# Column mean of an 8192 x 8192 matrix: an eight-row ring with two-row adds in place of five two-row slabs, and a head that comes uncast by the hardware queue

## The chip, the cores and the metric

The kernel runs on one core of one Trainium2 chip. The metric is the device time of one execution in microseconds, as the median of repeated executions.

## The reference

```python
def reference(x: np.ndarray) -> np.ndarray:
    return np.mean(x, axis=0)
```

`x` is an 8192 x 8192 fp32 matrix (268 MB) of normal random numbers. The result is one row of 8192 fp32 means. Each element of x is read once and added once, so the work is a stream from HBM with one addition for each element.

## The kernel before, in words

The 8192 rows of x are taken as 64 blocks of 128 rows ("rows" of the schedule, below). A block of 128 rows lies across the 128 partitions, with all 8192 columns along each partition. The sum over the rows is made in two steps: first the blocks are added elementwise, which leaves 128 partial sums per column, then TensorE multiplies with a vector of ones, which adds up the 128 partitions.

**Loads.** `load` (L87) fetches two blocks at a time with a DMA issued by GpSimd, which casts fp32 to bf16 on the way into a slab of 128 x 16384 bf16. Each partition takes two neighbouring rows of x, one contiguous run of 64 KB. There are five slabs (`bufs=5`), so a load waits until the slab of five loads earlier has been consumed.

**Adds.** `total` is a 128 x 8192 fp32 tile. It is cleared once (L56). VectorE adds every block to it with one `tensor_add` of 8192 elements per partition (L96), 61 times, two for each slab. The loop runs over 31 two-block loads; of the last of these VectorE takes only the first block.

**TensorE.** `add_chunks` (L76) adds a stretch of columns of a source into PSUM with a matmul whose weights are ones: `ones_b` for bf16 sources, `ones` for the fp32 `total`. `BLOCKS` divides the 8192 columns into seven blocks, each with one PSUM bank `acc`. A block (c0, w, g) has g chunks of w columns; chunk j goes to partitions 32 j to 32 j + 31 of the bank, that is, to its own group of 32 columns of the TensorE array. TensorE takes, in this order: the second block of the last two-block load; `total`; the last but one row block, loaded alone; and the last row block, loaded in six pieces of falling width (L136), 4096 columns to 128. The instructions stand in TensorE's queue in that order, and no later one passes an earlier one.

**Drains and stores.** When a piece of the last row block has been added, `drain` scales a bank by 1/8192 into `res`, on ScalarE for blocks 1, 3 and 5 (L113) and on VectorE for the others (L115). `store` writes it to HBM, on ScalarE's queue or on SyncE's (L125, and L123 for the last block).

Nothing here is planned by hand beyond the order of the program: each engine executes its own instructions in that order, and waits on semaphores for the tiles that it reads or overwrites.

Of the kernel before, what the change touches and what calls it, by code (L numbers as in the profile page):

```python
# [1 line left out]

# [4 lines left out]


@with_exitstack
def kernel(  # L10
    ctx: ExitStack,
    tc: tile.TileContext,
    x: bass.AP,
    out: bass.AP,
):

    nc = tc.nc
    P = nc.NUM_PARTITIONS
    R, C = x.shape
    F32, BF16 = mybir.dt.float32, mybir.dt.bfloat16
    assert (R, C) == (8192, 8192)
    inv_r = 1.0 / float(R)
    G = 4
    M = P // G
    K = 2  # L30
    N_GROUPS = R // (K * P)

    BLOCKS = [
        (0, 512, 4), (2048, 512, 4), (4096, 512, 4), (6144, 256, 4), (7168, 128, 4),
        (7680, 128, 3), (8064, 128, 1),
    ]

    const_pool = ctx.enter_context(tc.tile_pool(name="const", bufs=1))  # L40
    slab_pool = ctx.enter_context(tc.tile_pool(name="slab", bufs=5))
    sum_pool = ctx.enter_context(tc.tile_pool(name="sum", bufs=1))
    psum_pool = ctx.enter_context(
        tc.tile_pool(name="acc", bufs=1, space=bass.MemoryType.PSUM)
    )
    res_pool = ctx.enter_context(tc.tile_pool(name="res", bufs=1))

    ones = const_pool.tile([P, M], F32, tag="ones")
    nc.vector.memset(ones, 1.0)  # L49
    ones_b = const_pool.tile([P, M], BF16, tag="ones_b")  # L50
    nc.vector.memset(ones_b, 1.0)  # L51
    warm = const_pool.tile([P, M], F32, tag="warm")
    nc.scalar.mul(out=warm, in_=ones, mul=inv_r)  # L53

    total = sum_pool.tile([P, C], F32, tag="total")
    nc.vector.memset(total, 0.0)  # L56

    acc = [
        psum_pool.tile([P, 512], F32, name=f"acc{b}", tag=f"acc{b}")
        for b in range(len(BLOCKS))  # L60
    ]
    res = [
        res_pool.tile([P, w], F32, name=f"res{b}", tag=f"res{b}")
        for b, (_, w, _) in enumerate(BLOCKS)
    ]
    started = [[False] * g for _, _, g in BLOCKS]

    def add_chunks(src, lo, hi, b, cast=True, stop=False):

        c0, w, g = BLOCKS[b]  # L70
        for j in range(g):
            c = c0 + j * w
            if not lo <= c < hi:
                continue
            assert c + w <= hi
            nc.tensor.matmul(  # L76
                out=acc[b][j * M : (j + 1) * M, 0:w],
                lhsT=ones_b if cast else ones,
                rhs=src[:, c : c + w],
                start=not started[b][j],  # L80
                stop=stop,
            )
            started[b][j] = True

    def load(r0, k):
        t = slab_pool.tile([P, K * C], BF16, name="slab", tag="slab")
        nc.gpsimd.dma_start(  # L87
            out=t[:, 0 : k * C],
            in_=x[r0 : r0 + k * P, :].rearrange("(p k) c -> p (k c)", k=k),
        )  # L90
        return t

    for g in range(N_GROUPS - 1):
        t = load(g * K * P, K)
        for k in range(K if g < N_GROUPS - 2 else 1):
            nc.vector.tensor_add(out=total, in0=total, in1=t[:, k * C : (k + 1) * C])  # L96
    for b in range(len(BLOCKS)):
        add_chunks(t[:, C : 2 * C], 0, C, b)
    for b in range(len(BLOCKS)):
        add_chunks(total, 0, C, b, cast=False)  # L100
    t = load(R - K * P, 1)
    for b in range(len(BLOCKS)):
        add_chunks(t, 0, C, b)


    last = x[R - P : R, :]
    tb = slab_pool.tile([P, K * C], BF16, name="slab", tag="slab")

    def drain(b, eng):
        w = BLOCKS[b][1]  # L110
        rows = BLOCKS[b][2] * M
        if eng == "act":
            nc.scalar.mul(out=res[b][0:rows], in_=acc[b][0:rows, 0:w], mul=inv_r)  # L113
        else:
            nc.vector.tensor_scalar(  # L115
                out=res[b][0:rows], in0=acc[b][0:rows, 0:w], scalar1=inv_r, scalar2=None,
                op0=mybir.AluOpType.mult,
            )

    def store(b, q):  # L120
        lo, w, g = BLOCKS[b]
        if g == 1:
            q.dma_start(out=out[lo : lo + w], in_=res[b][0:1, :])  # L123
        else:
            q.dma_start(  # L125
                out=out[lo : lo + g * w].rearrange("(j w) -> j w", j=g),
                in_=res[b].rearrange("(j m) w -> j m w", m=M)[0:g, 0, :],
            )

    PIECES = ((0, 2), (2, 3), (3, 4), (4, 5), (5, 6), (6, 7))  # L130
    spans = []
    for b0, b1 in PIECES:
        lo = BLOCKS[b0][0]
        hi = BLOCKS[b1 - 1][0] + BLOCKS[b1 - 1][1] * BLOCKS[b1 - 1][2]
        spans.append((lo, hi))
        nc.gpsimd.dma_start(out=tb[:, lo:hi], in_=last[:, lo:hi])  # L136
    for (b0, b1), (lo, hi) in zip(PIECES, spans):
        for b in range(b0, b1):
            add_chunks(tb, lo, hi, b, stop=True)
            drain(b, "act" if b in (1, 3, 5) else "dve")  # L140
            store(b, nc.scalar if b in (1, 3, 5) else nc.sync)


# [1 line left out]
_INS = ['x']  # L145
_OUTS = [((8192,), 'float32')]


# [23 lines left out]
```

## Time and profile before

| | |
|---|---|
| median of 12 runs | 629.59 us (628.79 to 630.51) |
| the profiled execution's own time | 629.14 us |
| its span, first to last instruction | 627.3 us |
| VectorE busy | 539.2 us (86%), of it 61 adds of 8.69 us |
| TensorE busy | 11.0 us (2%) |
| GpSimd | 38 loads; HBM read 268.44 MB |
| granted TensorE clock | 0.998 |

The span is what the profile shows; the execution's own time also has 1.9 us around it. The page divides the span into 40 slices and gives for each engine its busy share in tenths, and for the DMA engines their mean busy share; it then follows the chain of work that ended last back to the start. In the timeline each line has a start, a duration, the engine, the line of the code and the operation, and in brackets how long the engine was idle before and what ended that.

### The profile page before, as it was taken

Reading aid. Unit: us, or ns where it says so; the run is one execution under the profiler, and the core shown is the slowest. Engines: PE = TensorE matmul, PEld = TensorE weight load, DVE = VectorE, ACT = ScalarE, POOL = GpSimd, SP = SyncE. Lnnn points to the kernel's source line nnn. Section 1 sums busy time; section 2 is a strip of 40 time slices with the busy share of each in tenths; the row PEclk is TensorE's granted clock in tenths of the full one; section 3 lists DMA queues with packets and bytes.
Section 4 is the critical chain, followed back from the end, with each engine's and each line's share of the span. In section 5 each row is a group of like instructions: output and inputs, shape, how many; then the busy total and the mean of one; then the engine's idle time right before and its main releaser. Section 6 shows DMA issues by size and latency. Waiting matters only on the chain.

```text
span 627.3 us, 466 instructions
## 1 busy us (share of the span) xinstructions
PE 11.0 (2%) x120; PEld 4.6 (1%) x120; DVE 539.2 (86%) x68; ACT 2.8 (0%) x5; POOL 20.4 (3%) x42
## 2 busy tenths in 40 slices
PE   0000000000000000000000000000000000000015
PEld 0000000000000000000000000000000000000002
DVE  4488988889888899888898888988889988899881
ACT  0000000000000000000000000000000000000000
POOL 1000000000000000000000000000000000000000
PEclk9999999999999999999999999999999999999999
DMA  9999999999999999999999999999999999999997
GB/s 190 211 219 215 217 217 211 224 211 224 209 226 207 228 205 230 201 234 201 234 201 234 201 234 201 235 201 234 201 234 201 234 201 234 201 235 201 234 200 138
DMA packets 5523, 134.29 MB, mean 214 GB/s; under 512 B 760, under 2 KB 1028, under 8 KB 1296
## 3 DMA queue, kind: packets, MB, share of 16 engines
q0 software_dynamic: 5472, 134.22, 99.7%
q1 hardware_dynamic: 26, 0.02, 0.0%
q8 instruction: 1, 0.02, 0.0%
q10 hardware_dynamic: 22, 0.01, 0.0%
q14 instruction: 2, 0.02, 0.0%
HBM read 268.44 MB, written 0.03 MB: 428 GB/s over the span
## 4 chain that ended last, share of the span: by engine, by line
DVE 82%; another core or an unknown queue 9%; DMA 7%; PE 1%; issue 1%; POOL 0%; DVEq 0%; POOLq 0%
DVE total L96 82%; DMA slab<-in_x_dram 7%; PE acc L76 1%; POOL slab L87 0%; DVEq L96 0%; DVE res L115 0%; POOLq L156 0%
## 5 line engine op out<-in xcount | busy, mean ns | idle before, releaser
L96 DVE TENSOR_TENSOR total<-total,slab 128x8192 f32<-128x8192 f32 x61 | 530.2, 8692 | 72.5 <-DMA slab<-in_x_dram 71.5
L87 POOL DMA_DIRECT2D slab<-in_x_dram x32 | 17.0, 535 | 527.0 <-DVE total L96 526.2
L76 PE MATMUL acc<-slab,ones_b 128*32 128x512 bf16 (+2 forms) x72 | 5.1, 369 | 606.4 <-DMA slab<-in_x_dram 606.4
L115 DVE TENSOR_SCALAR res<-acc 128x512 f32<-128x512 f32 (+2 forms) x4 | 2.0, 488 | 10.4 <-PE acc L76 10.3
L56 DVE MEMSET total<- 128x8192 f32 x1 | 6.9, 6885 | 1.7 <-issue 1.7
L76 PEld LDWEIGHTS <-ones_b 128*32 128x32 bf16 x72 | 2.8, 108 | 608.2 <-issue 606.8
L76 PE MATMUL acc<-total,ones 128*32 128x512 f32 (+2 forms) x48 | 6.4, 681 | 6.8 <-DVE total L96 6.8
L136 POOL DMA_DIRECT2D slab<-in_x_dram x6 | 3.2, 544 | 37.3 <-DVE total L96 18.8
L113 ACT ACTIVATE res<-acc 128x512 f32<-128x512 f32 (+2 forms) x3 | 1.3, 418 | 620.9 <-PE acc L76 620.9
L76 PEld LDWEIGHTS acc<-total,ones 128*32 128x32 f32 x48 | 2.0, 143 | 11.2 <-DVE total L96 7.1
L53 ACT ACT_TABLE_LOAD x1 | 1.3, 1283 | 0.7 <-PEq L156 0.7
L49 DVE MEMSET ones<- 128x32 f32 x1 | 0.1, 85 | 0.8 <-PEq L156 0.8
L53 ACT ACTIVATE warm<-ones 128x32 f32<-128x32 f32 x1 | 0.2, 229 | 0.0
L156 POOL MEMSET const-float32-0.0<- 128x1 f32 x1 | 0.1, 98 | 0.2 <-issue 0.2
L156 POOL MEMSET const-bfloat16-1.0<- 128x1 bf16 x1 | 0.1, 101 | 0.0
L156 POOL MEMSET const-float32-1.0<- 128x1 f32 x1 | 0.1, 98 | 0.0
L156 POOL MEMSET const-uint8-127<- 128x1 uint8 x1 | 0.1, 98 | 0.0
L51 DVE MEMSET ones_b<- 128x32 bf16 x1 | 0.1, 85 | 0.0
## 6 DMA issues: line engine op xcount, KB each, us to landing
slab<-in_x_dram POOLq DMA_DIRECT2D x31, 4096.0 KB, 78.8
slab<-in_x_dram POOLq DMA_DIRECT2D x1, 2048.0 KB, 69.2
slab<-in_x_dram POOLq DMA_DIRECT2D x1, 1024.0 KB, 54.7
slab<-in_x_dram POOLq DMA_DIRECT2D x1, 512.0 KB, 56.6
slab<-in_x_dram POOLq DMA_DIRECT2D x1, 256.0 KB, 57.4
slab<-in_x_dram POOLq DMA_DIRECT2D x1, 128.0 KB, 58.7
slab<-in_x_dram POOLq DMA_DIRECT2D x1, 96.0 KB, 58.4
slab<-in_x_dram POOLq DMA_DIRECT2D x1, 32.0 KB, 39.6
```

Source lines behind the costliest of these rows:

```text
L49: nc.vector.memset(ones, 1.0)
L51: nc.vector.memset(ones_b, 1.0)
L53: nc.scalar.mul(out=warm, in_=ones, mul=inv_r)
L56: nc.vector.memset(total, 0.0)
L76: nc.tensor.matmul(out=acc[b][j * M : (j + 1) * M, 0:w], lhsT=ones_b if cast else ones, rhs=src[:, c : c + w], start=not started[b][j], st ...
L87: nc.gpsimd.dma_start(out=t[:, 0 : k * C], in_=x[r0 : r0 + k * P, :].rearrange("(p k) c -> p (k c)", k=k),)
L96: nc.vector.tensor_add(out=total, in0=total, in1=t[:, k * C : (k + 1) * C])
L113: nc.scalar.mul(out=res[b][0:rows], in_=acc[b][0:rows, 0:w], mul=inv_r)
L115: nc.vector.tensor_scalar(out=res[b][0:rows], in0=acc[b][0:rows, 0:w], scalar1=inv_r, scalar2=None, op0=mybir.AluOpType.mult,)
L136: nc.gpsimd.dma_start(out=tb[:, lo:hi], in_=last[:, lo:hi])
L156: nc = _bacc.Bacc("TRN2", target_bir_lowering=False, num_devices=1)
```

## The change

- **Ring.** The slab pool is replaced by one tile `ring` of eight row blocks in bf16. Loads take consecutive places in it: eight loads of four blocks, fourteen of two, two of one (`LOADS`), then the last block in five pieces. A load waits until the places that it overwrites have been consumed.
- **Head.** The first row block comes first and alone. Its first 1024 columns are loaded as fp32 straight into `total` by two DMAs, one issued by SyncE and one by ScalarE, 64 partitions each. The other 7168 columns come by GpSimd as bf16 into place 7 of the ring, and ScalarE copies them into `total` (L98). The clearing of `total` and a warm-up activation on ScalarE are gone.
- **Two-row sum.** `total` is twice as wide, 128 x 16384 fp32. VectorE adds two row blocks with one `tensor_add` of 16384 elements per partition (L118), 27 times. The first four-block load makes the second half out of two blocks (L113) and adds the other two to the first half (L114, L115). Before the last two-block load that VectorE takes, the second half is added to the first (L122), and then the two blocks of that load one by one (L124).
- **TensorE's rows.** TensorE takes the two single-row loads and the last block: the first single row as it comes, then the first half of `total`, then the second single row (`late`), then the pieces of the last block.
- **Blocks.** `BLOCKS` has six entries in place of seven: three of 4 x 512 as before, then 2 x 512, 2 x 384 and 2 x 128. There are 18 chunks for each source instead of 24. TensorE's list of instructions has 116 rows where it had 153.
- **Stores.** Blocks 0 and 1 share a tile `res01` and one store on SyncE's queue (L169). Block 4 is stored from ScalarE's queue, the others from SyncE's (L148). Drains are at L139 (ScalarE: blocks 1, 3 and 4) and L141 (VectorE: blocks 0, 2 and 5); matmuls are at L86, loads at L97, L105 and L159.

```diff
-    K = 2
-    N_GROUPS = R // (K * P)
+    RING = 8
+    LOADS = [4] * 8 + [2] * 14 + [1] * 2
+    PE_ROWS = 2
+    HEADW = 1024
     BLOCKS = [
-        (0, 512, 4), (2048, 512, 4), (4096, 512, 4), (6144, 256, 4), (7168, 128, 4),
-        (7680, 128, 3), (8064, 128, 1),
+        (0, 512, 4), (2048, 512, 4), (4096, 512, 4), (6144, 512, 2), (7168, 384, 2),
+        (7936, 128, 2),
     ]
...
+    total = sum_pool.tile([P, 2 * C], F32, tag="total")
+    ring = ring_pool.tile([P, RING * C], BF16, tag="ring")
+    half = P // 2
+    nc.sync.dma_start(out=total[0:half, 0:HEADW], in_=x[0:half, 0:HEADW])
+    nc.scalar.dma_start(out=total[half:P, 0:HEADW], in_=x[half:P, 0:HEADW])
...
-    warm = const_pool.tile([P, M], F32, tag="warm")
-    nc.scalar.mul(out=warm, in_=ones, mul=inv_r)
-    total = sum_pool.tile([P, C], F32, tag="total")
-    nc.vector.memset(total, 0.0)
...
-    for g in range(N_GROUPS - 1):
-        t = load(g * K * P, K)
-        for k in range(K if g < N_GROUPS - 2 else 1):
-            nc.vector.tensor_add(out=total, in0=total, in1=t[:, k * C : (k + 1) * C])
-    for b in range(len(BLOCKS)):
-        add_chunks(t[:, C : 2 * C], 0, C, b)
-    for b in range(len(BLOCKS)):
-        add_chunks(total, 0, C, b, cast=False)
-    t = load(R - K * P, 1)
-    for b in range(len(BLOCKS)):
-        add_chunks(t, 0, C, b)
+    at = RING - 1
+    head = ring[:, at * C : (at + 1) * C]
+    nc.gpsimd.dma_start(out=head[:, HEADW:C], in_=x[0:P, HEADW:C])
+    nc.scalar.copy(out=total[:, HEADW:C], in_=head[:, HEADW:C])
+    lo_, hi_ = total[:, 0:C], total[:, C : 2 * C]
+    r0, at = P, 0
+    n_dve = len(LOADS) - PE_ROWS
+    for g, k in enumerate(LOADS):
+        t = ring[:, at * C : (at + k) * C]
+        nc.gpsimd.dma_start(
+            out=t,
+            in_=x[r0 : r0 + k * P, :].rearrange("(p k) c -> p (k c)", k=k),
+        )
+        r0 += k * P
+        at = (at + k) % RING
+        row = [t[:, i * C : (i + 1) * C] for i in range(k)]
+        if g == 0:
+            nc.vector.tensor_add(out=hi_, in0=row[1], in1=row[3])
+            nc.vector.tensor_add(out=lo_, in0=lo_, in1=row[0])
+            nc.vector.tensor_add(out=lo_, in0=lo_, in1=row[2])
+        elif g < n_dve - 1:
+            for i in range(0, k, 2):
+                nc.vector.tensor_add(
+                    out=total, in0=total, in1=t[:, i * C : (i + 2) * C]
+                )
+        elif g == n_dve - 1:
+            nc.vector.tensor_add(out=lo_, in0=lo_, in1=hi_)
+            for i in range(k):
+                nc.vector.tensor_add(out=lo_, in0=lo_, in1=row[i])
+        elif g == n_dve:
+            for b in range(len(BLOCKS)):
+                add_chunks(t, 0, C, b)
+        else:
+            late = t
...
-    PIECES = ((0, 2), (2, 3), (3, 4), (4, 5), (5, 6), (6, 7))
+    PIECES = ((0, 2), (2, 3), (3, 4), (4, 5), (5, 6))
...
+    for b in range(len(BLOCKS)):
+        add_chunks(lo_, 0, C, b, cast=False)
+    for b in range(len(BLOCKS)):
+        add_chunks(late, 0, C, b)
     for (b0, b1), (lo, hi) in zip(PIECES, spans):
         for b in range(b0, b1):
             add_chunks(tb, lo, hi, b, stop=True)
-            drain(b, "act" if b in (1, 3, 5) else "dve")
-            store(b, nc.scalar if b in (1, 3, 5) else nc.sync)
+            drain(b, "act" if b in (1, 3, 4) else "dve")
+            if b == 1:
+                nc.sync.dma_start(
+                    out=out[0 : 8 * 512].rearrange("(b j w) -> j b w", b=2, j=G),
+                    in_=res01.rearrange("(j m) b w -> j m b w", m=M)[:, 0, :, :],
+                )
+            elif b > 1:
+                store(b, nc.scalar if b == 4 else nc.sync)
```

## The prediction

> **What bounds the kernel now.** I read the page first, its slices and its chain of waits.
>
> ```profile
> DMA  9999999999999999999999999999999999999997
> PE 11.0 (2%) x120; PEld 4.6 (1%) x120; DVE 539.2 (86%) x68; ACT 2.8 (0%) x5; POOL 20.4 (3%) x42
> DVE 82%; another core or an unknown queue 9%; DMA 7%; PE 1%; issue 1%; POOL 0%; DVEq 0%; POOLq 0%
> L96 DVE TENSOR_TENSOR total<-total,slab 128x8192 f32<-128x8192 f32 x61 | 530.2, 8692 | 72.5 <-DMA slab<-in_x_dram 71.5
> ```
>
> The chain gives VectorE 82%, but that is only who stood in it: VectorE waits 71.5 us for slabs, and the DMA row is full to the last slice. The timeline of VectorE shows who sets the pace.
>
> ```profile
> 23.62 17.42 DVE L96 TENSOR_TENSOR total<-total,slab 128x8192 f32<-128x8192 f32 x2 [14.15 <-DMA slab<-in_x_dram]
> 42.90 17.42 DVE L96 TENSOR_TENSOR total<-total,slab 128x8192 f32<-128x8192 f32 x2 [1.86 <-DMA slab<-in_x_dram]
> ...
> 584.22 17.42 DVE L96 TENSOR_TENSOR total<-total,slab 128x8192 f32<-128x8192 f32 x2 [1.90 <-DMA slab<-in_x_dram]
> 603.53 8.69 DVE L96 TENSOR_TENSOR total<-total,slab 128x8192 f32<-128x8192 f32 x1 [1.89 <-DMA slab<-in_x_dram]
> ```
>
> From 42.90 to 603.53 lie 29 loads: 19.33 us for two row blocks ("rows" below: 128 rows of x, 4.19 MB), 9.66 us a row, 434 GB/s. VectorE needs 17.42 of each 19.33 us and idles 1.9. So **the loads bound the body**. The end is read from the timeline of TensorE, its weight loads and the stores.
>
> ```profile
> 612.27 0.20 PEld L76 LDWEIGHTS acc<-total,ones 128*32 128x32 f32 x8 [7.09 <-DVE total L96]
> 613.13 0.20 PEld L76 LDWEIGHTS acc<-total,ones 128*32 128x32 f32 x4 [0.66 <-issue]
> ...
> 617.40 0.88 PEld L76 LDWEIGHTS acc<-total,ones 128*32 128x32 f32 x19 [0.66 <-issue]
> 618.17 0.10 PEld L76 LDWEIGHTS <-ones_b 128*32 128x32 bf16 x3
> 619.86 0.69 DVE L115 TENSOR_SCALAR res<-acc 128x512 f32<-128x512 f32 x1 [7.63 <-PE acc L76]
> 620.07 0.60 ACT L113 ACTIVATE res<-acc 128x512 f32<-128x512 f32 x1 [617.81 <-PE acc L76]
> 623.64 0.60 PE L76 MATMUL acc<-slab,ones_b 128*32 128x128 bf16 x8 [1.61 <-DMA slab<-in_x_dram]
> 624.79 0.41 SPq L123 DMA_DIRECT2D out_dram<-res  x1
> ```
>
> VectorE's last add ends at 612.23, TensorE reduces `total` and the late row until about 619.3, and then still waits for the last pieces: the last lands at 623.6 and the span ends 3.7 us later (2.47 after the last store's issue at 624.79). VectorE was done 11.4 us before the last byte. **That slack hides its tail today**, and the change spends it.
>
> **What the Trainium skill says.** "VectorE: DVE Perf Modes", section on the TRN2 errata, prices an fp32 tensor_tensor at (N+151)/0.96 ns: 8.69 us for 8192, as the trace has it (8692 ns), so an estimated 17.22 us for 16384; its tier table keeps fp32 tensor_tensor at one element per cycle. "TensorE: Matmul & The Clock Gate", Part 1, has the array at half clock after idling and at full clock after some 3.4 us of work, with a free-running window. The trace agrees in kind: groups of four 512-wide fp32 passes start 0.855 us apart from 612.27 to 617.40; the eight 256-wide and sixteen 128-wide ones left, 1.71 us at that rate, start within 0.88. Here the switch came after 5.1 us. "DMA: Bandwidth & Descriptors", "Where 436 GB/s comes from", gives a ceiling of 435 GB/s; the trace has 434, so no load shape can gain much. Its "Specifications" gives a first byte after 1 us from GpSimd and 0.6 us from SP or ACT. The trace: GpSimd issues at 1.23 and the DMA share rises in the 2.5 to 2.6 window, 1.3 us; the last SP issue at 624.79 moves bytes in 625.8 to 625.9, 1.1 us.
>
> **The change, part by part.**
>
> *Start.* SP and ACT issue the first 1024 columns, 0.52 MB, 1.2 us of stream, by the hardware queue. They are free when the other engines start (ACT's table load at 0.73, VectorE at 0.81), so by 1.1 to 1.4 us later, bytes move at about 1.9 to 2.1 instead of 2.5. GpSimd's own first issue stays at 1.23. I take 0.6 us gained; the bounds are 0 (it starts no earlier) and 1.2 (the whole piece is hidden). The memset of `total` (6.9 us), the warm-up activation and its table load go: nothing, all lay under the first load's wait until 23.62. The new ScalarE copy of 7168 columns, at the 0.60 us per 512 of its evictions 8.4 us, starts when the head lands near 13 and ends near 21. GpSimd's third load waits for it, with every later load queued behind; but the first four-row load keeps the DMA engines busy until about 51, and the second add, which reads the copy, comes later still. Cost zero under that cover; with it gone, 8.4 us once.
>
> *Loads.* Same bytes, 30 GpSimd loads for 38. The 434 GB/s stands 0.3% under the ceiling, so fewer loads give between 0 and 0.4 us; I take 0. A four-row load (16.8 MB, two 64 KB runs per partition) shows nowhere in the trace; rate unchanged taken, 1% worse over 32 rows would be 3 us.
>
> *The ring in the four-row stage.* Before, five slabs; now two four-row halves. A half is freed 2 x 17.25 = 34.5 us after its load lands; the load in flight ends at 38.66. Cycle of a half: 34.5, 0.29 to GpSimd (VectorE ends 41.04, issue 41.34), 3.06 for a fresh start (1.23 to 23.62 less 19.33) and 38.66: 76.5 us against 77.3 for two loads of stream. **Slack 0.8 us**, cost zero. A doubled issue (0.53 more for twice the descriptors) still fits. The two-row loads have three loads of slack. VectorE, late when they begin, gains 2.1 us per load and has caught up by the ninth of 14.
>
> *The wide adds.* 61 x 8.69 = 530 us becomes 27 x 17.22 + 6 x 8.69 = 517 us. Covered by the loads: no gain.
>
> *The end of VectorE.* This is the term that counts. Now `total` is two rows wide and must be folded (L122), and three rows, not two, follow the last VectorE load. The second last two-row load completes row 59 of 64. Before, row 60 starts its add at 584.22; so row 59 at 584.22 - 9.66 - 0.6 = 573.96. Then one wide add 17.22, the fold 8.69, two adds of the last load 17.38 (it lands at 593.3, while the fold runs), gaps 0.14: 43.43 us, ending at **617.39, against 612.23**. TensorE's fp32 pass and, queued in order behind it, the late row and all the last pieces wait for that.
>
> *TensorE.* The fp32 pass shrinks from 24 to 18 matmuls of the same 8192 columns, but the last three blocks use two column groups, not four. Three blocks of 4x512 at half clock: 6 x 0.855 = 5.13 us, as before; then at full clock 2 x 0.427 for 512, 2 x 0.32 for 384, 2 x 0.11 for 128: 1.71. Sum 6.84, before 5.9. By when the clock rises (after 3.4 to 6.8 us), 6.0 to 7.7. From 617.43: ends 624.27. The late row takes 1.2 (618.17 to 619.3 before): the last pieces start at 625.5, all landed by about 623. They are not waited for any more.
>
> *Drains and stores.* Before, six pieces spread them; now they come together. After the start of the last pieces the first drain came 0.6 us later and ScalarE's 0.8: VectorE 626.1 (0.69), 626.8 (0.69), 627.5 (0.3); ScalarE 626.3 (0.6), 626.9 (0.6), 627.5 (0.5) and its store, issued at 628.1. SP issues four stores 0.54 us apart, the joint one from 626.95: the last at about 628.6. The end lies 2.47 later: **631.05, against 627.26: +3.8 us**. Fewer blocks and stores save nothing I can place, since the queue of drains sets the end.
>
> *Sum.* Start -0.6; VectorE's tail 43.43 less the 9.66 of one row and the 28.01 from row 60's start to 612.23, +5.8; TensorE's fp32 pass +0.9; from the late row's end to the span's end 5.55 us (625.5 to 631.05) for 8.0 (619.3 to 627.3), since no piece is waited for, -2.4: +3.7, 3.8 unrounded. The profiled execution took 629.14 (span 627.3 and 1.9 around it), 0.45 under the median 629.59. So 632.9 there, 633.4 at the median; I say 633.3.
>
> **The rivals.**
>
> *The ring starves (slower still).* If the first bytes of a four-row load come d us later than a two-row one's, each half's cycle overruns by d - 0.8, half of that per load, over six loads: d = 2 gives 3.6 us, 637. Or the longer runs stream 1% slower: 636. For it: 0.8 us is thin. Against: the issue takes only 0.53 us, the descriptors are of the size used now, and the queue is never empty at the hand-over. Chance 0.12.
>
> *The fold is cheap (not slower).* The fold's operands are all fp32, a form absent from the trace. If it ran at two elements per cycle, 4.35 us instead of 8.69, VectorE would end at 613.0 and the time fall to 633.3 - 4.35 = 629.0, 0.1% under before. It decides from 3.8 us off VectorE's 43.4. For it: nothing measured; against: the skill's tier table and the fp32 operand and result of today's adds at 8692 ns. Together with a full 1.2 us at the start it would be 628.4. Chance 0.08.
>
> *The hardware loads do not start earlier.* Then the head is plain: 633.9. It lies inside the forecast's range.
>
> **How the numbers follow.** Forecast 0.80, its own range 631.8 to 635.0 (start 0.6 either way, clock 0.85, stores 0.5). Starving 0.12, cheap fold 0.08. About 0.2% (1.26 us) is what a measurement of this kernel can tell from no change; the cheap fold splits into 0.04 faster and 0.04 the same, and the rest of the cases are slower; I move 0.02 more to no change for a lucky sum of bounds: faster 0.04, same 0.06, slower 0.90. The range 631.2 to 636.8 holds the forecast and most of the starving case.
>
> **What would show it.** Right: the fold at 8.7 us and wide adds at 17.2; the last add ending near 617.4; TensorE's fp32 pass beginning then and its last pieces waiting for no DMA; the last store's issue near 628.6; in the four-row stage a DMA share near 1 and landings 38.7 us apart; first bytes near 2.0. Wrong: gaps in the DMA share when two halves change over, a fold near 4.4 us, or a last VectorE add before 613, with TensorE again waiting for the last pieces.

## Result and the profile after

The changed kernel takes **636.53 us** (median, 635.48 to 636.82) against 629.55: 1.0107 of the time before, 95% interval 1.0098 to 1.0117. That is slower by 7.0 us, where 3.7 were forecast; the direction holds, and so does the wide range (631.2 to 636.8), but only because most of the starving case was taken into it: the forecast's own range, 631.8 to 635.0, does not hold 636.53. The profiled execution took 637.36 us, 0.8 above the median, with a span of 635.2.

The page of the changed kernel, its DMA row, the hardware queues and the group of wide adds:

```profile
DMA  9999999999999999999999999999999999999994
...
q1 hardware_dynamic: 108, 0.29, 0.2%
q10 hardware_dynamic: 84, 0.27, 0.1%
...
L118 DVE TENSOR_TENSOR total<-total,ring 128x16384 f32<-128x16384 f32 x27 | 465.1, 17225 | 52.8 <-DMA ring<-in_x_dram 52.3
```

The DMA row looks as full as before; why the loss does not show there is said below the table of issues. The wide add takes 17.225 us, as estimated. The loss is found in the timeline of VectorE (start, duration, and in brackets how long it waited):

```profile
52.69 8.69 DVE L113 TENSOR_TENSOR total<-ring 128x8192 f32<-128x8192 bf16 x1 [51.75 <-DMA ring<-in_x_dram]
...
91.37 34.48 DVE L118 TENSOR_TENSOR total<-total,ring 128x16384 f32<-128x16384 f32 x2 [12.66 <-DMA ring<-in_x_dram]
129.95 34.48 DVE L118 TENSOR_TENSOR total<-total,ring 128x16384 f32<-128x16384 f32 x2 [4.10 <-DMA ring<-in_x_dram]
170.34 34.48 DVE L118 TENSOR_TENSOR total<-total,ring 128x16384 f32<-128x16384 f32 x2 [5.91 <-DMA ring<-in_x_dram]
209.01 34.48 DVE L118 TENSOR_TENSOR total<-total,ring 128x16384 f32<-128x16384 f32 x2 [4.18 <-DMA ring<-in_x_dram]
249.89 34.49 DVE L118 TENSOR_TENSOR total<-total,ring 128x16384 f32<-128x16384 f32 x2 [6.39 <-DMA ring<-in_x_dram]
288.48 34.49 DVE L118 TENSOR_TENSOR total<-total,ring 128x16384 f32<-128x16384 f32 x2 [4.11 <-DMA ring<-in_x_dram]
328.15 172.56 DVE L118 TENSOR_TENSOR total<-total,ring 128x16384 f32<-128x16384 f32 x10 [5.18 <-DMA ring<-in_x_dram]
...
579.39 17.23 DVE L118 TENSOR_TENSOR total<-total,ring 128x16384 f32<-128x16384 f32 x1 [2.12 <-DMA ring<-in_x_dram]
596.65 8.69 DVE L122 TENSOR_TENSOR total<-total 128x8192 f32<-128x8192 f32 x1
605.38 17.42 DVE L124 TENSOR_TENSOR total<-total,ring 128x8192 f32<-128x8192 f32 x2
```

A four-row load streams in 38.66 us, twice the 19.33 of a two-row one. The steps between the starts are 38.6, 40.4, 38.7, 40.9, 38.6 and 39.7: three of the six come late, by 1.7, 2.2 and 1.0 us, 5.0 in all. (In a line with x2 or x10 only the first add waited.) The issues of these loads, from GpSimd's timeline:

```profile
126.15 0.71 POOL L105 DMA_DIRECT2D ring<-in_x_dram  x1 [46.44 <-DVE total L118]
164.74 0.70 POOL L105 DMA_DIRECT2D ring<-in_x_dram  x1 [37.88 <-DVE total L118]
205.12 0.71 POOL L105 DMA_DIRECT2D ring<-in_x_dram  x1 [39.69 <-DVE total L118]
243.80 0.70 POOL L105 DMA_DIRECT2D ring<-in_x_dram  x1 [37.96 <-DVE total L118]
284.67 0.71 POOL L105 DMA_DIRECT2D ring<-in_x_dram  x1 [40.17 <-DVE total L118]
```

Each waits for VectorE to free its half of the ring. Set beside the start of the add that belongs to the load ahead of it, "lead" is how long before that start it was issued:

| issued | load ahead: add starts | lead, us | own add starts | late by, us |
|---|---|---|---|---|
| 126.15 | 129.95 | 3.80 | 170.34 | 1.7 |
| 164.74 | 170.34 | 5.60 | 209.01 | 0.0 |
| 205.12 | 209.01 | 3.89 | 249.89 | 2.2 |
| 243.80 | 249.89 | 6.09 | 288.48 | -0.1 |
| 284.67 | 288.48 | 3.81 | 328.15 | 1.0 |

Short leads come late, long ones do not; and a late load gives the next one a longer lead, which is why every other one suffers. The lead alone does not fix the size of the delay. e4 and e6, below, keep these loads and this ring; in their traces and this one together, nine loads were issued with a lead of 3.8 to 4.2 us, and they came 0.1 to 2.2 us late. With 5.5 us and more none of the three traces has a late one.

The trace also has the single packets, and a landing event from each of the 16 DMA engines for every load. In the running stream a packet of 32 KB takes 2.43 us on its engine. At the first late hand-over all engines begin their first packet of the new load at once (128.54 to 129.59), but these sixteen packets take 2.4 to 4.3 us, 3.1 in the median. In e7, where the lead is longer, the same sixteen take 2.43. So at this hand-over the engines are slow rather than idle, and a slow packet counts as busy: the DMA share is 1.05 from 126 to 136 and 0.99 in the ten us after. (At the third one they also stood idle; from 284 to 294 the share is 0.85.) Nor are all engines hit alike. Between the landings before the first and after the third late hand-over (129.86 and 328.06), the mean of the sixteen lost 3.8 us and the last of them, for which VectorE waits, 4.9. From there to the end of the stream the last engine trails the first by 2.2 us; up to the first late hand-over it was 1.0.

The end, from the timelines of TensorE and its weight loads, VectorE, ScalarE and SP's queue:

```profile
622.85 0.20 PEld L86 LDWEIGHTS acc<-total,ones 128*32 128x32 f32 x8 [12.59 <-DVE total L124]
...
624.56 0.19 PEld L86 LDWEIGHTS acc<-total,ones 128*32 128x32 f32 x4 [0.66 <-issue]
625.42 0.19 PEld L86 LDWEIGHTS acc<-total,ones 128*32 128x32 f32 x4 [0.66 <-issue]
625.99 0.12 PEld L86 LDWEIGHTS acc<-total,ones 128*32 128x32 f32 x4 [0.38 <-issue]
...
628.46 0.28 PE L86 MATMUL acc<-total,ones 128*32 128x128 f32 x2
...
630.09 1.48 DVE L141 TENSOR_SCALAR res<-acc 128x512 f32<-128x512 f32 x3 [7.29 <-PE acc L86]
630.30 1.45 ACT L139 ACTIVATE res<-acc 128x512 f32<-128x512 f32 x3 [610.14 <-PE acc L86]
...
631.64 1.66 SPq L148 DMA_DIRECT2D out_dram<-res  x3
```

VectorE's tail from 579.39 to 622.81 is 43.42 us (43.43 worked out). Afterwards no matmul waits for a piece, and the drains run one behind the other, as forecast. From VectorE's end to the span's end are 12.4 us, 1.3 less than the 13.65 worked out. Most of this is the fp32 pass: its last matmuls start at 628.46, 5.6 us after the first, where 6.84 was worked out for the whole. The array came to full clock after some 3 us (the groups lie 0.86 us apart up to 625.42 and 0.57 from there to 625.99) and not after 5.1.

### The profile page after: what moved, and what is told of

It reads as the page before. It is cut to its first block, busy times and chain, and to the rows that moved or that the text cites. A ratio compares the mean times of both kernels' runs of the same rounds, so it can differ in the third digit from the quotient of the medians.

```text
span 635.2 us, 356 instructions
## 1 busy us (share of the span) xinstructions
PE 10.4 (2%) x90; PEld 3.6 (1%) x90; DVE 518.7 (82%) x38; ACT 8.9 (1%) x5; POOL 17.6 (3%) x34
## 4 chain that ended last, share of the span: by engine, by line
DVE 64%; DMA 21%; another core or an unknown queue 12%; issue 2%; PE 1%; ACT 0%; DVEq 0%
DVE total L118 57%; DMA ring<-in_x_dram 21%; DVE total L124 3%; DVE total L122 1%; DVE total L114 1%; DVE total L115 1%; PE acc L86 1%; ACT res L139 0%; DVEq L118 0%; DVE ones L62 0%; DVE total L113 0%; DVE ones_b L64 0%
## 5 line engine op out<-in xcount | busy, mean ns | idle before, releaser
L118 DVE TENSOR_TENSOR total<-total,ring 128x16384 f32<-128x16384 f32 x27 | 465.1, 17225 | 52.8 <-DMA ring<-in_x_dram 52.3
L113 DVE TENSOR_TENSOR total<-ring 128x8192 f32<-128x8192 bf16 x1 | 8.7, 8691 | 51.8 <-DMA ring<-in_x_dram 51.8
L105 POOL DMA_DIRECT2D ring<-in_x_dram x24 | 14.1, 589 | 543.3 <-DVE total L118 467.6
L124 DVE TENSOR_TENSOR total<-total,ring 128x8192 f32<-128x8192 f32 x2 | 17.4, 8693 | 0.1
L86 PE MATMUL acc<-ring,ones_b 128*32 128x512 bf16 (+2 forms) x54 | 5.2, 431 | 608.4 <-DMA ring<-in_x_dram 608.4
L139 ACT ACTIVATE res<-acc 128x512 f32<-128x512 f32 (+2 forms) x3 | 1.4, 551 | 610.1 <-PE acc L86 610.1
L115 DVE TENSOR_TENSOR total<-total,ring 128x8192 f32<-128x8192 f32 x1 | 8.7, 8692 | 0.0
L122 DVE TENSOR_TENSOR total<-total 128x8192 f32<-128x8192 f32 x1 | 8.7, 8692 | 0.0
L114 DVE TENSOR_TENSOR total<-total,ring 128x8192 f32<-128x8192 f32 x1 | 8.7, 8684 | 0.0
L141 DVE TENSOR_SCALAR res<-acc 128x512 f32<-128x512 f32 (+1 forms) x3 | 1.5, 547 | 7.3 <-PE acc L86 7.3
L98 ACT CAST total<-ring 128x7168 f32<-128x7168 bf16 x1 | 6.2, 6164 | 11.3 <-DMA ring<-in_x_dram 11.3
L86 PE MATMUL acc<-total,ones 128*32 128x512 f32 (+2 forms) x36 | 5.9, 715 | 12.1 <-DVE total L124 12.1
L86 PEld LDWEIGHTS <-ones_b 128*32 128x32 bf16 x54 | 2.2, 107 | 610.4 <-issue 609.4
L159 POOL DMA_DIRECT2D ring<-in_x_dram x5 | 2.6, 548 | 18.3 <-DVE total L118 18.3
L86 PEld LDWEIGHTS acc<-total,ones 128*32 128x32 f32 x36 | 1.6, 138 | 16.6 <-DVE total L124 12.6
L97 POOL DMA_DIRECT2D ring<-in_x_dram x1 | 0.7, 667 | 0.8 <-POOLq L189 0.8
```

The costliest lines, as they stand in the source:

```text
L86: nc.tensor.matmul(out=acc[b][j * M : (j + 1) * M, 0:w], lhsT=ones_b if cast else ones, rhs=src[:, c : c + w], start=not started[b][j], st ...
L98: nc.scalar.copy(out=total[:, HEADW:C], in_=head[:, HEADW:C])
L105: nc.gpsimd.dma_start(out=t, in_=x[r0 : r0 + k * P, :].rearrange("(p k) c -> p (k c)", k=k),)
L113: nc.vector.tensor_add(out=hi_, in0=row[1], in1=row[3])
L114: nc.vector.tensor_add(out=lo_, in0=lo_, in1=row[0])
L115: nc.vector.tensor_add(out=lo_, in0=lo_, in1=row[2])
```

## The experiments

Theory A: the four-row loads are issued too late. Theory D: VectorE's late end, with the fold and two adds behind the last landing, is exposed. Rivals: the shape of a four-row load (B), the head or the ring tile (C), the loads alone (E). All results are medians; each ratio is to the kernel before on the same chip.

| kernel | us | ratio, 95% interval |
|---|---|---|
| changed kernel | 636.53 | 1.0107 (1.0098 to 1.0117) |
| e1, two-row loads | 632.63 | 1.0054 (1.0039 to 1.0069) |
| e2, TensorE takes a fourth row | 633.22 | 1.0066 (1.0051 to 1.0081) |
| e3, two-row loads, ring of four rows | 681.02 | one run |
| e4, early fold | 633.63 | 1.0068 (1.0051 to 1.0085) |
| e5, e1 and e4 together | 628.54 | 0.9983 (0.9977 to 0.9990) |
| e6, no hardware loads | 635.70 | 1.0098 (1.0084 to 1.0111) |
| e7, TensorE takes a quarter row | 633.02 | 1.0057 (1.0043 to 1.0071) |
| e8, e5 without hardware loads | 628.58 | 0.9986 (0.9979 to 0.9992) |
| e9, kernel before with the new end | 628.82 | 0.9986 (0.9980 to 0.9993) |

### e1: two-row loads in the same ring

```diff
-    LOADS = [4] * 8 + [2] * 14 + [1] * 2
+    LOADS = [2] * 30 + [1] * 2
...
         if g == 0:
-            nc.vector.tensor_add(out=hi_, in0=row[1], in1=row[3])
             nc.vector.tensor_add(out=lo_, in0=lo_, in1=row[0])
-            nc.vector.tensor_add(out=lo_, in0=lo_, in1=row[2])
+        elif g == 1:
+            nc.vector.tensor_add(out=hi_, in0=prev, in1=row[1])
+            nc.vector.tensor_add(out=lo_, in0=lo_, in1=row[0])
...
+        prev = row[-1]
```

> The changed kernel with LOADS of thirty two-row loads in place of eight four-row and fourteen two-row ones; ring, head, wide adds, fold and TensorE's rows stay. Theory A (a four-row load is issued too late before the DMA queues run dry, because the ring then holds only two of them): the 5.0 us lost on the landings of the fourth, sixth and eighth load go, nothing else moves; the last wide add starts near 574.4 instead of 579.4, and the time is about 631.5 us. Theory B (a load of four rows costs more by its shape, two runs per partition and 256 descriptors): the same 631.5. Theory C (the loss belongs to the hardware head or to the ring tile, not to the four-row loads): it stays at 636.5.

The timeline of VectorE in e1, at the same wide add as 579.39 above and after it:

```profile
574.45 17.23 DVE L119 TENSOR_TENSOR total<-total,ring 128x16384 f32<-128x16384 f32 x1 [2.16 <-DMA ring<-in_x_dram]
591.71 8.69 DVE L123 TENSOR_TENSOR total<-total 128x8192 f32<-128x8192 f32 x1
600.43 17.42 DVE L125 TENSOR_TENSOR total<-total,ring 128x8192 f32<-128x8192 f32 x2
```

574.45, against 574.4 expected: the whole loss on the landings is gone. The time is 632.63, 1.1 us over the expectation: the expectation took the 5.0 us of a profiled execution that lay 0.8 over its median off that median; the rest is in the end, 12.85 us from VectorE's last add (617.85) to the end of the span (630.7) instead of 12.4. C falls; A and B are not told apart by this. Beside its own kernel before (629.35), e1 is 3.3 us slower: without the loss on the landings, the change costs about what the prediction made of it (3.7).

### e2 and e7: the same four-row loads, freed earlier

```diff
+        elif k == 4:
+            nc.vector.tensor_add(out=total, in0=total, in1=t[:, 0 : 2 * C])
+            nc.vector.tensor_add(out=lo_, in0=lo_, in1=row[2])
+            for b in range(len(BLOCKS)):
+                add_chunks(row[3], 0, C, b)
```

> The changed kernel with the same loads, but in the seven later four-row loads TensorE adds the fourth row straight into PSUM and VectorE adds three (one wide add and one single), so that a half of the ring is freed about 8.5 us earlier (26 us after landing instead of 34.5). Theory A (late issue): every four-row load is then issued some 12 us before the queues run dry, landings come 38.66 us apart, and the time is about 631.5. Theory B (shape of the four-row load): the loss of 5 us stays, 636.5.

In e7 the fourth row is shared: VectorE adds its first 6144 columns and `add_chunks(row[3], 6144, C, b)` takes the rest.

> The changed kernel with the same loads; in the seven later four-row loads TensorE adds only the last 2048 columns of the fourth row, so that a half of the ring is freed about 2 us earlier than in the changed kernel. There, loads issued 3.8 to 3.9 us before the load ahead landed came 1.0 to 2.2 us late, and loads issued 5.6 or 6.1 us before came in time. Theory A with a threshold between (lead decides): leads become 5.8 us, nearly the whole loss goes, about 633.0. Rival (the loss falls in proportion to the work taken from VectorE, a quarter of what e2 took): 635.7.

GpSimd's timeline in e7, two of the issues:

```profile
124.28 0.71 POOL L105 DMA_DIRECT2D ring<-in_x_dram  x1 [44.74 <-DVE total L119]
162.88 0.70 POOL L105 DMA_DIRECT2D ring<-in_x_dram  x1 [37.89 <-DVE total L119]
```

VectorE's timeline in e7, the adds that start each four-row load:

```profile
129.80 17.23 DVE L117 TENSOR_TENSOR total<-total,ring 128x16384 f32<-128x16384 f32 x1 [6.04 <-DMA ring<-in_x_dram]
...
168.43 17.23 DVE L117 TENSOR_TENSOR total<-total,ring 128x16384 f32<-128x16384 f32 x1 [6.08 <-DMA ring<-in_x_dram]
...
207.11 17.23 DVE L117 TENSOR_TENSOR total<-total,ring 128x16384 f32<-128x16384 f32 x1 [6.14 <-DMA ring<-in_x_dram]
```

The lead is now 129.80 - 124.28 = 5.5 us, and the starts lie 38.6 and 38.7 apart, none late. e7 gives 633.02, where A, with e1 and e2 known, had 633.0 and the rival 635.7. e2, with 12 us of lead and TensorE's whole row, gives no more: 633.22, 1.7 over the 631.5 expected, which took off the same 5.0 us as in e1 (the intervals of e1, e2 and e7 overlap). **B falls as the main cause: the same load shape costs nothing when it is issued 1.7 us earlier.** The profiled execution of e2 was its slowest of four (634.49, the others 632.9 to 633.4) and still has three steps that are 0.3 to 1.0 us too long in spite of the lead. In the third (285.75) a single DMA engine fell behind by 1.0 us; a likely reason comes with e9. The first two, 0.4 and 0.3 us, hit all sixteen alike and stay open.

### e3: two-row loads issued as late

```diff
-    RING = 8
-    LOADS = [4] * 8 + [2] * 14 + [1] * 2
+    RING = 4
+    LOADS = [2] * 30 + [1] * 2
```

The first adds are as in e1.

> Two-row loads throughout and a ring of four rows in place of eight, so that two-row loads are issued as late as the four-row loads are now: 17.25 us after a landing, 1.8 us before the other load lands. Theory A, with the fresh start that the changed kernel shows (126.15 to 170.34 less 38.66, 5.5 us): two loads take 17.25 + 0.29 + 5.5 + 19.33 = 42.4 us instead of 38.66, over 30 loads some 55 us more, about 687. With the 3.06 us of the prediction: 39.9, about 650. Theory B (only the four-row shape is slow): about 632.

GpSimd's timeline in e3, three issues of the running stream:

```profile
287.80 0.53 POOL L105 DMA_DIRECT2D ring<-in_x_dram  x1 [22.14 <-DVE total L119]
307.69 0.53 POOL L105 DMA_DIRECT2D ring<-in_x_dram  x1 [19.36 <-DVE total L119]
327.38 0.53 POOL L105 DMA_DIRECT2D ring<-in_x_dram  x1 [19.16 <-DVE total L119]
```

VectorE's timeline in e3, the adds around them:

```profile
290.17 17.23 DVE L119 TENSOR_TENSOR total<-total,ring 128x16384 f32<-128x16384 f32 x1 [2.66 <-DMA ring<-in_x_dram]
309.86 17.23 DVE L119 TENSOR_TENSOR total<-total,ring 128x16384 f32<-128x16384 f32 x1 [2.46 <-DMA ring<-in_x_dram]
332.37 17.23 DVE L119 TENSOR_TENSOR total<-total,ring 128x16384 f32<-128x16384 f32 x1 [5.28 <-DMA ring<-in_x_dram]
352.22 17.23 DVE L119 TENSOR_TENSOR total<-total,ring 128x16384 f32<-128x16384 f32 x1 [2.62 <-DMA ring<-in_x_dram]
```

681.0 us in one run, 6 under A's 687 and far from 632 and 650: two-row loads starve as well when they are issued late. The steps are 19.7, 22.5 and 19.9 for a stream of 19.33, and through the middle of the run the pattern of three repeats. Leads of 2.2 and 2.4 us cost 3.2 and 0.4: so the lead alone is not a law for a single load here, only for the row of them. The landings of the single engines show why. The load that VectorE saw 0.4 us late, at 309.86, was 3.2 late in the mean of its sixteen engines; but one engine had been trailing by 3 us, and that one lost nothing. With the next load it is the other way round: 0.9 us in the mean, 3.2 on the last engine.

### e4 and e5: the fold five loads earlier

```diff
-        elif g < n_dve - 1:
+        elif g < FOLD_AT:
...
-        elif g == n_dve - 1:
-            nc.vector.tensor_add(out=lo_, in0=lo_, in1=hi_)
+        elif g < n_dve:
+            if g == FOLD_AT:
+                nc.vector.tensor_add(out=lo_, in0=lo_, in1=hi_)
             for i in range(k):
                 nc.vector.tensor_add(out=lo_, in0=lo_, in1=row[i])
```

`FOLD_AT` is `n_dve - 6`. e5 has this edit and that of e1.

> The changed kernel with the fold of the two halves of total five loads earlier (before the adds of the seventeenth load), and single-row adds from there on; the loads are unchanged. Theory D (VectorE's late end is exposed: fold and two adds after the last landing): the last add ends near 616.1 instead of 622.8, TensorE again waits for the last pieces (landing at 627.5 in the changed kernel), the span ends 3.7 us after them, 631.2, and the time is about 632.5. Rival E (the late loads alone set the end): 636.5 as the changed kernel.

> Both repairs together: two-row loads throughout (as in e1) and the fold five loads earlier (as in e4). Theory A+D (late four-row loads and VectorE's exposed end are the whole loss): VectorE ends near 611, the last pieces land near 622.6 as in e1, the span ends 3.7 to 4.0 later at 626.5, and the time is about 628.4, 1 us under the kernel before. Rival: with the loads repaired the end in e1 was already set by something else than VectorE's fold (drains, stores): 632.6 as e1.

The timeline of TensorE in e4:

```profile
616.26 6.99 PE L86 MATMUL acc<-total,ones 128*32 128x512 f32 x32 [5.83 <-DVE total L126]
...
626.27 0.39 PE L86 MATMUL acc<-ring,ones_b 128*32 128x512 bf16 x2 [0.85 <-DMA ring<-in_x_dram]
627.23 0.58 PE L86 MATMUL acc<-ring,ones_b 128*32 128x384 bf16 x4 [0.56 <-DMA ring<-in_x_dram]
```

VectorE releases TensorE at 616.26 (616.1 expected), TensorE waits for pieces again, and the span ends at 631.2: D holds and E falls. The time is 633.63, 1.1 over the expectation: the span's surroundings took 2.3 us in that execution where 1.9 were reckoned, and the 0.6 us that the expectation took off, since a profiled execution had lain above its median, did not come off here (633.54 against 633.63). The two repairs take 3.9 and 2.9 us alone, and 8.0 together: each alone leaves the other's term at the end of the path. e5 gives 628.54 (628.4 expected), **below the kernel before by 0.17%** (0.10 to 0.23).

### e6 and e8: no hardware loads

```diff
-    HEADW = 1024
+    HEADW = 0
-    nc.sync.dma_start(out=total[0:half, 0:HEADW], in_=x[0:half, 0:HEADW])
-    nc.scalar.dma_start(out=total[half:P, 0:HEADW], in_=x[half:P, 0:HEADW])
```

> The changed kernel without the two hardware loads: GpSimd's first load takes all 8192 columns of the head, ScalarE copies them all. Theory F (the hardware loads gain nothing: their 0.52 MB run from 2.09 to about 4.0 and push GpSimd's first bytes from 2.6 to 3.84, by as much as the head is shorter): the first four-row load's add starts at 52.6 to 52.8 as now (52.69), and the time stays within 0.5 us of 636.5. Rival (they gain the 0.6 us of the prediction): 637.1.

> e5 without the two hardware loads. Theory F (they gain nothing): the same as e5, 628.4, within 0.3 us. Rival (0.6 us gained by them): 629.0.

Stretches of the changed kernel's start (the two last columns are DMA share and GB/s; a packet counts where it begins, so a burst of large ones reads over 1):

```profile
1.80:2.00 0.20, 0.00 (x0) 0.00 (x0) 0.00 (x0) 0.20 (x1) 0.20 (x2) 1.00 0.00 0
2.00:2.20 0.20, 0.00 (x0) 0.00 (x0) 0.00 (x0) 0.20 (x1) 0.20 (x1) 1.00 0.57 123
...
3.50:3.80 0.30, 0.00 (x0) 0.00 (x0) 0.00 (x0) 0.00 (x0) 0.00 (x0) 1.00 0.81 328
3.80:4.00 0.20, 0.00 (x0) 0.00 (x0) 0.00 (x0) 0.00 (x0) 0.00 (x0) 1.00 2.08 584
```

The hardware loads move bytes from about 2.0, as expected, but slowly: SP's packets begin at 2.1 and ScalarE's at 3.2. GpSimd's large packets begin only near 3.8, where in the kernel before and in e6 they begin at 2.6: 1.2 us later, as much as the head is shorter. VectorE's timeline in e6:

```profile
52.56 8.69 DVE L111 TENSOR_TENSOR total<-ring 128x8192 f32<-128x8192 bf16 x1 [51.63 <-DMA ring<-in_x_dram]
...
129.96 34.49 DVE L116 TENSOR_TENSOR total<-total,ring 128x16384 f32<-128x16384 f32 x2 [4.20 <-DMA ring<-in_x_dram]
168.71 34.48 DVE L116 TENSOR_TENSOR total<-total,ring 128x16384 f32<-128x16384 f32 x2 [4.27 <-DMA ring<-in_x_dram]
208.32 34.48 DVE L116 TENSOR_TENSOR total<-total,ring 128x16384 f32<-128x16384 f32 x2 [5.13 <-DMA ring<-in_x_dram]
```

Its first four-row add starts at 52.56, the changed kernel's at 52.69. e5 and e8 are alike (628.54, 628.58), and e6 is no slower than the changed kernel: 635.70 lies 0.3 us outside the half microsecond of theory F, on the side away from the rival. The head is worth nothing. (The load that starts at 168.71 was issued at 126.05, 3.9 us ahead of 129.96, and came 0.1 us late. Over the seven steps between four-row loads, e6's profiled execution loses 2.6 us and the changed kernel's 4.8.) That the loads of all queues run on the same DMA engines and interleave is what the Trainium skill says ("DMA: Bandwidth & Descriptors", "Issuing engines are not separate DMA queues"), and the traces agree: with the hardware loads GpSimd's first packets come at 3.8, without them at 2.6.

### e9: the kernel before with the new end

```diff
-        (0, 512, 4), (2048, 512, 4), (4096, 512, 4), (6144, 256, 4), (7168, 128, 4),
-        (7680, 128, 3), (8064, 128, 1),
+        (0, 512, 4), (2048, 512, 4), (4096, 512, 4), (6144, 512, 2), (7168, 384, 2),
+        (7936, 128, 2),
...
-    PIECES = ((0, 2), (2, 3), (3, 4), (4, 5), (5, 6), (6, 7))
+    PIECES = ((0, 2), (2, 3), (3, 4), (4, 5), (5, 6))
```

with the drains and the joint store of the change.

> The kernel before with only the end of the change: six blocks in place of seven, five last pieces in place of six, the joint store of blocks 0 and 1; slabs, adds and VectorE's last load as before. It asks where the 1 us lies by which e5 is under the kernel before (628.5 against 629.5). Theory G (the end: in the kernel before the last piece lands 1.4 us after the first of its 16 engines is done, in e5 0.8 us): 628.6. Rival (the body: fewer and wider loads or adds): 629.5.

In e9 TensorE's matmuls on the last two pieces start at 622.77, where the kernel before started its last ones at 623.64 (shown with the prediction); the timeline of e9:

```profile
622.77 0.61 PE L78 MATMUL acc<-slab,ones_b 128*32 128x384 bf16 x4 [0.59 <-DMA slab<-in_x_dram]
```

628.82: by the medians 0.65 us of e5's 1.0 come from this end alone, by the ratios 0.14% of 0.17%, and the intervals of e5 and e9 overlap. The end gains, then, wherever it waits for the last pieces. Which part of it gains is not shown, since e9 changes blocks, pieces, drains and the joint store together.

The traces point to a cause that theory G does not name. In the kernel before, the last piece is complete on its first DMA engine at 622.27 and on its last at 623.98, 1.7 us later (the expectation had 1.4); in e9 at 622.35 and 623.05. In the kernel before that distance was still 0.8 us for the piece that landed at 621.70. At 621.57 begins a packet of 16 KB that carries instructions and takes 0.96 us; from the next piece on, one engine trails. The page of the kernel before has it among its DMA queues:

```profile
q8 instruction: 1, 0.02, 0.0%
```

e9 has no such packet. e7 has one, at 621.23, and there one engine falls from 0.8 to 1.9 us behind although the end is the new one. e2 has one at 250.45, in the load that then landed 1.0 us late on one engine. The pages of these three kernels (before, e7, e2) count 120, 132 and 216 matmuls; the eight kernels without the packet have 90 each. So it is probably TensorE's shorter list, which does without this fetch, that gains, and not the number of pieces. No run changed the list alone, so this stays argued.

## Why the prediction was right or wrong

- **The end of VectorE: right.** The tail of 43.43 us measured 43.42, the fold took 8.69 and the wide add 17.225; taking the fold out of the tail (e4) takes 2.9 us off. With the landings repaired the fold at the end costs some 4 us (e1 against e5). The cheap fold, the rival on the other side, did not occur.
- **The ring: wrong.** The step "Slack 0.8 us, cost zero" is the one that failed. Its term of 3.06 us for a fresh start was taken from the first load of all, which ran alone. In the stream a load issued with 3.8 us of lead landed 44.2 us later (126.15 to 170.34), 5.5 over its 38.66; over the nine loads with such leads in the three traces it is 4.0 to 6.1. With 5.5 for 3.06 the cycle of a half is 79.0 us against 77.3. Measured, 5.0 us were lost in the profiled execution and some 4 at the median. The sign that the prediction named for it, gaps in the DMA share, hardly shows, because slow packets count as busy.
- **The starving rival: the right place, the number by luck.** It had 0.12, and its 637 is near what came, but it rests on a freely chosen 2 us for four-row loads alone. e3 shows that two-row loads starve too: it is not the width of the load but the lateness of its issue, and a single late issue cost from 0.1 to 2.2 us.
- **The start: wrong by 0.6 us.** First bytes came at 2.0, as said, but they delayed GpSimd's; the lower bound of 0 was the right value. ScalarE's copy took 6.2 us, not the estimated 8.4, and was covered, as said.
- **TensorE: mis-sized by 1.3 us.** 12.4 us from VectorE's end to the span's for 13.65. The fp32 pass took 5.6 to 5.9 us (its last two matmuls start at 628.46), under the lower bound of 6.0. The prediction took the rise of the clock to come between 3.4 and 6.8 us; it came after some 3. The skill's window of about 3.4 us of sustained work runs freely, so that the moment may vary ("TensorE: Matmul & The Clock Gate", Part 1); 5.1 us before is within what the prediction took from it, and some 3 here is below, so the measurement decides.
- **Sum.** Forecast span 631.05, + 5.0 ring + 0.6 start - 1.3 TensorE = 635.4, measured 635.2. The ring's 5.0 is read off the result, so the sum shows that nothing large is missing and not that it could have been forecast.

## What to carry to other kernels

When two large buffers replace several small ones, take the lead of each issue over the end of the stream ahead from the timeline, and price a late issue from a load in the running stream, not from the first one; here a lead of 5.5 us kept the stream whole (e7), and one of 3.8 to 4.2 cost 0.1 to 2.2 us a load. Work that is folded or merged at the end of a reduction belongs some loads earlier, where the stream covers it. A DMA row full of nines says that the engines are busy, not that they move at full rate: read the distances between landings.

## What was not expected of the hardware

- A load issued 3.8 to 4.2 us before the one ahead was used came 0.1 to 2.2 us late, though its issue on GpSimd took only 0.7 us; at 5.5 us none did. Its first packets begin on time and are slow: up to 4.3 us for 2.43. The first packets of the first load of the kernel before, which ran alone, took 2.7 to 3.5. What slows them, and why the hand-over in the running stream needs more than the 3.06 us of a lone first load, stays open.
- A packet of 16 KB with instructions, in the stream, is followed each time (the kernel before, e2, e7) by one DMA engine of the sixteen falling about 1 us behind the others, and the load is as late as this one engine.
- After one late load the next is in time and the one after it late again: the loss alternates (38.6, 40.4, 38.7, 40.9, 38.6, 39.7), and with two-row loads in a ring of four it runs in threes.
- 0.52 MB by the hardware queues, in 4 KB rows, gained nothing at the start although it moved 0.5 us earlier.
